# A hybrid attention encoder block: one 128-row transfer for each Q head, both key copies taken from the rotary tile

## The chip, the core and the metric

The kernel runs on one core of one Trainium2 chip. A core has a matrix engine (TensorE, PE in the profile, with its weight loads as PEld), a vector engine (DVE), a scalar engine (ACT), GpSimd (POOL) and SyncE (SP), which here only issues transfers. Sixteen DMA engines carry the transfers. The metric is the device time of one execution in microseconds (us), as the median of several runs.

## The reference, cut to what matters

One encoder layer of width 1024 over 512 tokens and 16 learned meta tokens (528 positions). All arithmetic is float32.

```python
u = rms_norm(h, pre_mix_gain[l])
proj = u @ w_in[l]
qa, ka, va, qb, kb, vb, g = jnp.split(proj, SPLITS, axis=-1)
qa = rope(qa.reshape(B, Lp, SWA_Q_HEADS, HEAD_DIM), pos)     # 16 heads of 64
ka = rope(ka.reshape(B, Lp, SWA_KV_HEADS, HEAD_DIM), pos)    # 4 key heads
qb = rope(qb.reshape(B, Lp, DIFF_HEADS, 2, HEAD_DIM), pos)   # 8 heads of 2 x 64
kb = rope(kb.reshape(B, Lp, DIFF_HEADS, 2, HEAD_DIM), pos)
o_swa = windowed_gqa_sink_attention(qa, ka, va, attn_sink[l], pos, is_real)
o_diff = differential_attention(qb, kb, vb, lam, lambda_init, diff_subln_gain[l], is_key)
gates = jax.nn.sigmoid(g + b_gate[l])
merged = g_swa * (o_swa @ w_branch_swa[l]) + g_diff * (o_diff @ w_branch_diff[l])
h = h + rms_norm(merged @ w_out[l], post_mix_gain[l])
u = rms_norm(h, pre_ffn_gain[l])
gate_up = u @ w_ffn_in[l]
f = (jax.nn.silu(gate_up[..., :D_FF]) * gate_up[..., D_FF:]) @ w_ffn_out[l]
h = h + rms_norm(f, post_ffn_gain[l])
```

The rotary embedding `rope` splits the 64 channels of a head into two halves of 32 and returns `x1*cos - x2*sin` and `x2*cos + x1*sin`. The windowed attention gives each query the keys within 128 positions, the meta keys and a sink logit. The differential attention subtracts one softmax from another over all keys.

## The kernel before, in words

To keep float32 accuracy every operand of a matmul is split into a high part and a rest (`hi`, `lo`), and a product is three matmuls: hi by hi, lo by hi, hi by lo (lines 286 to 288, `mm3`). A projection of 128 output channels over 512 tokens is 8 blocks of the contraction, so 24 matmuls, into one of three PSUM banks named `pr`. Its weights come as one transfer of 512 KB into `wr` (line 519), are cast to `wh` on ACT (L521) and subtracted to `wl` on DVE or POOL (L252).

For the attention scores the split is folded into the contraction: a head has 64 channels, a score matmul contracts over 128 rows, so the Q tile holds 128 rows, the hi and the lo part of each of the two rotary halves (4 blocks of 32 rows), and K holds the same key channels twice, once under the hi rows of Q and once under the lo rows, with a second index x for the hi and lo part of K. Two matmuls (x = 0, 1) give the score.

These rows come about as follows. `rope_t` (line 539) makes a tile `hl` for four heads at once: partition 32*head + channel, then the rotary half i, the part (hi or lo) and the token. DVE makes the products `ta` and `tb` (L546), POOL adds them (L558), ACT writes the hi part (L554), DVE the lo part (L550). There is one `hl` buffer, so the next rotary tile may write it only when all transfers out of it have landed. Then `move` (line 567) copies rows from SBUF to SBUF on SP's queue into K and Q:

- windowed keys, for each of 4 key heads: two transfers of 32 rows into the lower 64 rows of `KK`, and then one of 64 rows that copies `KK[0:64]` to `KK[64:128]`;
- windowed Q (`q_swa`, four groups of four heads): four transfers of 32 rows and 64 KB for each head;
- differential attention (`qk`, 8 heads of 2 components): for each component the same, two transfers of 32 rows and a copy of 64 rows for `Kd`, four transfers of 32 rows for `Qd`.

The order of the work from the projections to the end of the differential attention is a plan. Each step is entered as a task with its engine, a cost, the tiles that it reads and writes, and a priority (`Plan.task`). `Plan.run` goes through time and gives each engine the next ready task; what it emits is the engine's instruction order, which the hardware then follows. Within the plan a transfer costs SP 0.6 us and is done 2.7 us later (`land`; 4.0 for the copies of 64 rows), and two transfers into the same tile follow one another there; on the chip they don't wait for each other. Projection matmuls have the lowest rank for PE (`prio` from 20 up) and fill it wherever no attention step is ready. The tile pools have fixed counts: three `wr`, one `hl`, four `kk` (keys), eight `q`.

The attention stage runs from some 25 us to some 525 us of the span. In it the windowed attention (16 units of one query block of four heads: `s_swa`, scores into `Sw` at line 705 and softmax; `t_swa`, transposes at 754 and values into `O` at 761 and 764) comes first, then the differential attention (`s_diff`, scores into `Sd` at 853; `t_diff`). The output projections and the feed-forward part follow, in an order that the change doesn't touch.

Of the kernel before, what the change touches and what calls it, by code (L numbers as in the profile page):

```python
# [12 lines left out]
F32 = mybir.dt.float32  # L13
F32R = mybir.dt.float32r
# [222 lines left out]
def encoder(ctx, tc, I, out, dbg=None):  # L237
# [300 lines left out]

    def rope_t(hl, pa, pb, c0, n, p0, o0, scale, more=False):

# [8 lines left out]
        def low(o, n):  # L549
            dve.scalar_tensor_tensor(out=hl.t[:, :, 1, o:o + n], in0=ta.t[:, :, 0:n], scalar=scale,  # L550
                                     in1=hl.t[:, :, 0, o:o + n].bitcast(F32), op0=ALU.mult, op1=ALU.subtract)

        def high(o, n):
            act.activation(out=hl.t[:, :, 0, o:o + n], in_=ta.t[:, :, 0:n], func=AF.Copy, scale=scale)  # L554

# [11 lines left out]
    def move(out, in_, r, w, dep=(), land=2.7):  # L567
        return T("SP", 0.6, lambda: sp.dma_start(out=out().bitcast(F32), in_=in_().bitcast(F32)), r=r, w=w, dep=dep,
                 prio=2, land=land)

    X_ = []
# [78 lines left out]
    for g in range(4):  # L650
        K = sb("kk", [P, 2, KX], F32R, "KK", 4, zp)
        for i in range(2):
            move(lambda i=i, K=K: K.t[32 * i:32 * i + 32], lambda i=i, g=g: hk.t[32 * g:32 * g + 32, i], [hk], [K])
        move(lambda K=K: K.t[64:128], lambda K=K: K.t[0:64], [], [K], land=4.0)
        KB.append(K)
# [15 lines left out]
    def q_swa(g):  # L671
        dep = Ssteps[4 * g - 8][:1] if g >= 2 else ()
        wa, wb = weights(I["w_in"][4 + 2 * g], dep), weights(I["w_in"][5 + 2 * g], dep)
        late = Ssteps[4 * g - 7][-1:] if g >= 2 else ()
        pa, pb = products(wa, X, X_, NMETA, EXT, late), products(wb, X, X_, NMETA, EXT, late)
        hl = sb("hl", [P, 2, 2, KX], F32R, "hl", 1, zp)
        for s in range(2):
            rope_t(hl, pa, pb, NMETA + s * 256, 256, s * 256, s * 256, -0.125)
        QS[g] = [sb("q", [P, EXT], F32R, "Q", 8) for _ in range(4)]
        for hh in range(4):  # L680
            for i in range(2):
                for c in range(2):
                    b = 2 * c + i
                    move(lambda hh=hh, b=b: QS[g][hh].t[32 * b:32 * b + 32, 0:NTOK],
                         lambda hh=hh, i=i, c=c: hl.t[32 * hh:32 * hh + 32, i, c, 0:NTOK], [hl], [QS[g][hh]])

# [106 lines left out]
    def qk(h):  # L793
# [4 lines left out]
        wa, wb = weights(I["w_in"][12 + 3 * h], early), weights(I["w_in"][13 + 3 * h], early)  # L798
        hl = sb("hl", [P, 2, 2, KX], F32R, "hl", 1, zp)
        for s in range(2):  # L800
# [4 lines left out]
        for c in range(2):  # L805
            K = sb("kk", [P, 2, EXT], F32R, "Kd", 4, zp)
            Q = sb("q", [P, EXT], F32R, "Qd", 8)
            for i in range(2):
                move(lambda i=i, K=K: K.t[32 * i:32 * i + 32], lambda i=i, c=c: hl.t[64 + 32 * c:96 + 32 * c, i, :, 0:EXT],
                     [hl], [K])  # L810
            move(lambda K=K: K.t[64:128], lambda K=K: K.t[0:64], [], [K], land=4.0)
            for i in range(2):
                for x in range(2):
                    b = 2 * x + i
                    hd["moved"] = move(lambda b=b, Q=Q: Q.t[32 * b:32 * b + 32, 0:NTOK],
                         lambda i=i, x=x, c=c: hl.t[32 * c:32 * c + 32, i, x, NMETA:EXT], [hl], [Q])
            hd["Q"].append(Q)
            hd["K"].append(K)
# [59 lines left out]

    lnx, dd, results, B1 = [], [], [], []

    def t_diff(h):
# [4 lines left out]
        for kb in range(5):  # L886
# [17 lines left out]
            def high(kb=kb, ah=ah):  # L904
                for x in range(2):
                    pe.matmul(out=O.t, lhsT=V.t[:, x, kb], rhs=ah.t, start=(kb == 0 and x == 0), stop=False)  # L906
            hd["Av"].append(T("PE", 2 * mm_t(512), high, r=[ah, V], w=[O], prio=0))
            hd["Av"].append(T("PE", mm_t(512), lambda kb=kb, al=al: pe.matmul(
# [3 lines left out]
        ob, sq, sh, sl = rt("ob"), rt("sq"), rt("sh", F32R), rt("sl", F32R)  # L912
        T("ACT", 0.59, lambda: act.copy(out=ob.t, in_=O.t), r=[O], w=[ob], prio=0)
        T("ACT", 0.61, lambda: act.activation(out=sq.t, in_=O.t, func=AF.Square), r=[O], w=[sq], prio=0)
        T("ACT", 0.63, lambda: act.copy(out=sh.t, in_=sq.t), r=[sq], w=[sh], prio=2)
# [3 lines left out]
        def sums():  # L919
            pe.matmul(out=mp.t, lhsT=ones, rhs=sh.t, start=True, stop=False)  # L920
            pe.matmul(out=mp.t, lhsT=ones, rhs=sl.t, start=False, stop=True)
        T("PE", 2 * mm_t(512), sums, r=[sh, sl], w=[mp], prio=0)
        v, y, z = rt("v"), rt("y"), rt("z")
# [6 lines left out]
        T("ACT", 0.63, lambda: lnx.append(act.activation(out=y.t, in_=y.t, func=AF.Exp, scale=-0.5)), w=[y], prio=4)  # L930
        T("ACT", 0.63, lambda: act.activation(out=z.t, in_=y.t, func=AF.Square), r=[y], w=[z], prio=4)
        T("DVE", 0.69, lambda: dve.scalar_tensor_tensor(out=z.t, in0=z.t, scalar=-0.5, in1=v.t, op0=ALU.mult, op1=ALU.mult),
# [508 lines left out]
```

## Time and profile before

| | |
|---|---|
| median of 3 runs | 963.73 us (962.97 to 965.36) |
| the profiled execution: time | 965.27 us |
| the profiled execution: span from the first to the last instruction | 963.5 us |
| mean granted TensorE clock | 0.996 |
| busy: PE, PEld, DVE, ACT, POOL | 943.4, 844.1, 670.3, 504.3, 216.2 us |
| transfers | 109.43 MB, DMA engines busy 37.4% of the span |

The profile's page gives busy times, a timeline of 40 slices, a chain of waits that ended last, and groups of instructions. Further views are used below: who waited for whom; instructions in order of time; busy time by stretch, with the granted clock, the share of time in which the DMA engines were busy and what they moved; and transfers with the time from issue to landing. Times inside a view count from the start of the span. PE's ends are modelled, so a matmul's duration overlaps its successor; the distance between two starts is what a matmul costs.

### The profile page before, as it was taken

What the parts mean: (1) busy time and instruction counts of PE and PEld (TensorE: products, weight loads), DVE (VectorE), ACT (ScalarE), POOL (GpSimd) and SP (SyncE); (2) the same over time, 40 slices, a digit from 0 to 9 for tenths busy, and PEclk for the clock granted to TensorE, in tenths of its full rate; (3) what the DMA queues carried; (4) which work ended last, traced back from release to release, by engine and by line L of the source; (5) the groups of instructions that cost most, each with busy time, mean ns of one, the idle gap of its engine ahead of it and who ended that gap; (6) DMA issues with size and microseconds to landing.
All of it is one profiled execution on the core that took longest, in us unless ns stands there. A gap on an engine that the chain in (4) does not pass through costs nothing.

```text
span 963.5 us, 15670 instructions
## 1 busy us (share of the span) xinstructions
PE 943.4 (98%) x5919; PEld 844.1 (88%) x5919; DVE 670.3 (70%) x1202; ACT 504.3 (52%) x939; POOL 216.2 (22%) x228
## 2 busy tenths in 40 slices
PE   9898999999999999999999999999999999999996
PEld 9787878889898999999888888998999999988885
DVE  5836898999574759877774857877788788752224
ACT  6336676775644446667546433744555556632121
POOL 0543455543222323234212311300000000000000
PEclk9999999999999999999999999999999999999998
DMA  9483222251425144433531551444333332324122
GB/s 338 139 194 90 77 77 70 73 134 48 130 88 155 45 124 121 129 84 107 159 118 45 185 186 44 132 154 153 91 114 104 110 111 68 109 88 152 44 66 88
DMA packets 37147, 109.43 MB, mean 114 GB/s; under 512 B 6080, under 2 KB 6592, under 8 KB 37072
## 3 DMA queue, kind: packets, MB, share of 16 engines
q1 hardware_dynamic: 37072, 108.43, 37.4%
q8 instruction: 47, 0.77, 0.3%
q14 instruction: 28, 0.23, 0.1%
HBM read 87.04 MB, written 2.10 MB: 93 GB/s over the span
## 4 chain that ended last, share of the span: by engine, by line
PE 88%; DVE 5%; DMA 2%; ACT 1%; SPq 1%; issue 1%; DVEq 0%; ACTq 0%
PE pr L286 19%; PE pr L287 19%; PE pr L288 19%; PE Sd L853 3%; PE wk L287 2%; PE wk L288 2%; PE wk L286 2%; PE Sw L705 2%; PE O L761 2%; PE tr L893 2%; PE Od L906 2%; PE tr L288 2%; PE tr L287 2%; PE tr L286 2%; PE tr L754 2%; PE acc L288 1%
## 5 line engine op out<-in xcount | busy, mean ns | idle before, releaser
L286 PE MATMUL pr<-xh,wh 128*128 128x264 f32 (+1 forms) x616 | 199.9, 325 | 0.0
L288 PE MATMUL pr<-xh,wl 128*128 128x264 f32 (+1 forms) x616 | 196.5, 319 | 0.3 <-POOL wl L252 0.3
L287 PE MATMUL pr<-xl,wh 128*128 128x264 f32 (+1 forms) x616 | 196.6, 319 | 0.1
L252 POOL TENSOR_TENSOR wl<-wr,wh 128x1024 fp32r<-128x1024 f32 (+2 forms) x42 | 99.8, 2377 | 141.3 <-ACT wh L521 78.0
L252 DVE TENSOR_TENSOR wl<-wr,wh 128x1024 fp32r<-128x1024 f32 (+2 forms) x76 | 91.5, 1208 | 53.5 <-ACT wh L271 43.7
L288 PEld LDWEIGHTS pr<-xh,wl 128*128 128x128 f32 x616 | 116.0, 188 | 8.9 <-POOL wl L252 0.5
L287 PEld LDWEIGHTS pr<-xl,wh 128*128 128x128 f32 x616 | 116.2, 189 | 7.9 <-DVE xl L393 0.5
L286 PEld LDWEIGHTS pr<-xh,wh 128*128 128x128 f32 x616 | 116.3, 189 | 7.3
L521 ACT CAST wh<-wr 128x1024 fp32r<-128x1024 f32 x56 | 58.5, 1049 | 42.1 <-PE pr L287 34.5
L271 ACT CAST wh<-wr 128x1024 fp32r<-128x1024 f32 x44 | 46.2, 1052 | 65.3 <-PE pr L288 17.9
L308 POOL TENSOR_TENSOR r3y<-r3v,mhalf 128x1 f32<-128x1 f32 x4 | 2.2, 548 | 336.8 <-DVE r3v L307 336.8
L286 PE MATMUL pr<-TM,sx 128*128 128x256 f32 x240 | 68.1, 284 | 0.9 <-ACT u L1272 0.5
L287 PE MATMUL pr<-TM,sx 128*128 128x256 f32 x240 | 67.9, 283 | 0.0
L288 PE MATMUL pr<-TM,sx 128*128 128x256 f32 x240 | 67.9, 283 | 0.0
L858 DVE TENSOR_REDUCE nm<-Sd 128x1 f32<-128x528 f32 x64 | 45.1, 705 | 21.0 <-PE Sd L853 20.1
L288 PE MATMUL pr<-uh,wl 128*128 128x256 f32 (+1 forms) x200 | 59.2, 296 | 0.4 <-DVE wl L252 0.4
L286 PE MATMUL pr<-uh,wh 128*128 128x256 f32 (+1 forms) x200 | 59.3, 296 | 0.0
L287 PE MATMUL pr<-ul,wh 128*128 128x256 f32 (+1 forms) x200 | 59.1, 296 | 0.0
L252 DVE TENSOR_TENSOR sx<-S,sx 128x1024 fp32r<-128x1024 f32 x34 | 41.6, 1225 | 25.1 <-PE wk L287 12.7
L558 POOL TENSOR_TENSOR ta<-ta,tb 128x528 f32<-128x528 f32 (+1 forms) x26 | 36.5, 1402 | 79.1 <-DVE tb L546 59.3
L256 ACT CAST sx<-S 128x1024 fp32r<-128x1024 f32 x34 | 35.7, 1050 | 25.8 <-PE pr L288 8.1
L861 ACT ACTIVATE pp<-Sd,nm 128x528 f32<-128x528 f32 x40 | 28.0, 699 | 39.2 <-DVE pa L874 22.6
(401 smaller groups left out, 2550.1 us busy)
## 6 DMA issues: line engine op xcount, KB each, us to landing
wr<-in_w_in_dram SPq DMA_DIRECT2D x50, 512.0 KB, 4.2
wr<-in_w_fo_dram SPq DMA_DIRECT2D x22, 512.0 KB, 3.5
wg<-in_w_fi_dram SPq DMA_DIRECT2D x17, 512.0 KB, 3.6
wu<-in_w_fi_dram SPq DMA_DIRECT2D x17, 512.0 KB, 3.6
wr<-in_w_fi_dram SPq DMA_DIRECT2D x16, 512.0 KB, 4.2
Kd<-hl SPq DMA_DIRECT2D x32, 132.0 KB, 2.4
Kd<-Kd SPq DMA_DIRECT2D x16, 264.0 KB, 3.6
Q<-hl SPq DMA_DIRECT2D x64, 64.0 KB, 2.7
```

What stands on the lines that cost most here:

```text
L252: (eng or dve).tensor_tensor(out=lo, in0=src, in1=hi.bitcast(F32), op=ALU.subtract)
L256: act.copy(out=hi, in_=src)
L271: act.copy(out=wh, in_=raw)
L286: pe.matmul(out=ps, lhsT=ah, rhs=bh, start=first, stop=False, **more)
L287: pe.matmul(out=ps, lhsT=ah, rhs=bl, start=False, stop=False, **more)
L288: pe.matmul(out=ps, lhsT=al, rhs=bh, start=False, stop=last, **more)
L521: T("ACT", 1.05, lambda: act.copy(out=wh.t, in_=wr.t), r=[wr], w=[wh], prio=pr_)
L558: T("POOL", 0.05 + 1.3 * m, lambda: pool.tensor_tensor(out=ta.t[:, :, 0:n], in0=ta.t[:, :, 0:n], in1=tb.t[:, :, 0:n], op=ALU.add), r=[tb], ...
L705: pe.matmul(out=Sw2[S.slot][:, 0:nk], lhsT=QS[g][hh].t[:, i * P:(i + 1) * P], rhs=KB[g].t[:, x, r0:r1], start=(x == 0), stop=(x == 1))
L853: pe.matmul(out=S.t[:, s, 0:HALF], lhsT=Q[c].t[:, i * P:(i + 1) * P], rhs=K[c].t[:, x, s * HALF:(s + 1) * HALF], start=(x == 0), stop=(x = ...
L858: T("DVE", 0.71, lambda S=S, c=c, one=one: dve.tensor_reduce(out=nm.t[:, c, one], in_=S.t[:, :, 0:HALF], axis=AX.XY, op=ALU.min), r=[S], w ...
L861: T("ACT", 0.9, lambda S=S, c=c, one=one, p=p: act.activation(out=p().rearrange("p (a b) -> p a b", a=2), in_=S.t[:, :, 0:HALF], func=AF.E ...
```

## The change

It does four things.

1. In `q_swa` the rotary tile is laid out with the part (hi, lo) ahead of the rotary half (`hi_first`), so that the four pieces of a channel lie behind each other, and a head's Q becomes one transfer: 32 partitions of four pieces of 2 KB in the source, 128 rows of 2 KB in the destination. Row 4p + 2a + b of Q then holds piece (a, b) of channel p. In `qk` the same is done with the half ahead of the part.
2. Both copies of the windowed keys are written straight from `hl`. For each half i one transfer writes the 64 rows i, i+2, i+4, ... of `KK`; its source of 32 rows is read twice over (a broadcast). The copy from `KK` to `KK` is gone: per key head two transfers instead of three.
3. For the differential keys four transfers of 32 rows, each into every fourth row, replace two of 32 rows and the copy of 64. The tile `hl` is 528 wide there instead of 544, so a source row is contiguous (4224 bytes instead of two pieces of 2112).
4. In `t_diff` three tasks get further dependencies in the plan: the value matmuls of a head come after the previous head's `mp` matmuls, and the two ACT reads of `Od` after the previous head's last `z`. They bound the plan's order.

The plan's costs for a transfer stay as they were (0.6 us and 2.7 us to landing), so the plan itself comes out differently, and the order of instructions on all engines between the projections and the end of the differential attention with it.

```diff
-    def rope_t(hl, pa, pb, c0, n, p0, o0, scale, more=False):
+    def rope_t(hl, pa, pb, c0, n, p0, o0, scale, more=False, hi_first=False):
+
+        def part(x):
+            return hl.t[:, x] if hi_first else hl.t[:, :, x]
...
-            dve.scalar_tensor_tensor(out=hl.t[:, :, 1, o:o + n], in0=ta.t[:, :, 0:n], scalar=scale,
-                                     in1=hl.t[:, :, 0, o:o + n].bitcast(F32), op0=ALU.mult, op1=ALU.subtract)
+            dve.scalar_tensor_tensor(out=part(1)[:, :, o:o + n], in0=ta.t[:, :, 0:n], scalar=scale,
+                                     in1=part(0)[:, :, o:o + n].bitcast(F32), op0=ALU.mult, op1=ALU.subtract)
...
+    def move_q(Q, src, r):
+        return move(lambda: Q.t[:, 0:NTOK], lambda: src().rearrange("p a b c -> p (a b) c"), r, [Q])
...
         K = sb("kk", [P, 2, KX], F32R, "KK", 4, zp)
         for i in range(2):
-            move(lambda i=i, K=K: K.t[32 * i:32 * i + 32], lambda i=i, g=g: hk.t[32 * g:32 * g + 32, i], [hk], [K])
-        move(lambda K=K: K.t[64:128], lambda K=K: K.t[0:64], [], [K], land=4.0)
+            move(lambda K=K, i=i: K.t[i::2].rearrange("p x c -> p (x c)"),
+                 lambda g=g, i=i: hk.t[32 * g:32 * g + 32, i].rearrange("p x c -> p (x c)").unsqueeze(1).broadcast_to(
+                     [32, 2, 2 * KX]), [hk], [K])
...
-            rope_t(hl, pa, pb, NMETA + s * 256, 256, s * 256, s * 256, -0.125)
+            rope_t(hl, pa, pb, NMETA + s * 256, 256, s * 256, s * 256, -0.125, hi_first=True)
         QS[g] = [sb("q", [P, EXT], F32R, "Q", 8) for _ in range(4)]
         for hh in range(4):
-            for i in range(2):
-                for c in range(2):
-                    b = 2 * c + i
-                    move(lambda hh=hh, b=b: QS[g][hh].t[32 * b:32 * b + 32, 0:NTOK],
-                         lambda hh=hh, i=i, c=c: hl.t[32 * hh:32 * hh + 32, i, c, 0:NTOK], [hl], [QS[g][hh]])
+            move_q(QS[g][hh], lambda hh=hh: hl.t[32 * hh:32 * hh + 32, :, :, 0:NTOK], [hl])
...
-        hl = sb("hl", [P, 2, 2, KX], F32R, "hl", 1, zp)
+        hl = sb("hl", [P, 2, 2, EXT], F32R, "hl", 1, zp)
...
             for i in range(2):
-                move(lambda i=i, K=K: K.t[32 * i:32 * i + 32], lambda i=i, c=c: hl.t[64 + 32 * c:96 + 32 * c, i, :, 0:EXT],
-                     [hl], [K])
-            move(lambda K=K: K.t[64:128], lambda K=K: K.t[0:64], [], [K], land=4.0)
-            for i in range(2):
-                for x in range(2):
-                    b = 2 * x + i
-                    hd["moved"] = move(lambda b=b, Q=Q: Q.t[32 * b:32 * b + 32, 0:NTOK],
-                         lambda i=i, x=x, c=c: hl.t[32 * c:32 * c + 32, i, x, NMETA:EXT], [hl], [Q])
+                for a in range(2):
+                    move(lambda K=K, i=i, a=a: K.t[2 * i + a::4], lambda i=i, c=c: hl.t[64 + 32 * c:96 + 32 * c, i],
+                         [hl], [K])
+            hd["moved"] = move_q(Q, lambda c=c: hl.t[32 * c:32 * c + 32, :, :, NMETA:EXT], [hl])
...
-            hd["Av"].append(T("PE", 2 * mm_t(512), high, r=[ah, V], w=[O], prio=0))
+            hd["Av"].append(T("PE", 2 * mm_t(512), high, r=[ah, V], w=[O], dep=ms[-1:], prio=0))
...
-        T("ACT", 0.59, lambda: act.copy(out=ob.t, in_=O.t), r=[O], w=[ob], prio=0)
-        T("ACT", 0.61, lambda: act.activation(out=sq.t, in_=O.t, func=AF.Square), r=[O], w=[sq], prio=0)
+        T("ACT", 0.59, lambda: act.copy(out=ob.t, in_=O.t), r=[O], w=[ob], dep=zs[-1:], prio=0)
+        T("ACT", 0.61, lambda: act.activation(out=sq.t, in_=O.t, func=AF.Square), r=[O], w=[sq], dep=zs[-1:], prio=0)
...
-        T("PE", 2 * mm_t(512), sums, r=[sh, sl], w=[mp], prio=0)
+        ms.append(T("PE", 2 * mm_t(512), sums, r=[sh, sl], w=[mp], prio=0))
...
-        T("ACT", 0.63, lambda: act.activation(out=z.t, in_=y.t, func=AF.Square), r=[y], w=[z], prio=4)
+        zs.append(T("ACT", 0.63, lambda: act.activation(out=z.t, in_=y.t, func=AF.Square), r=[y], w=[z], prio=4))
```

The instruction orders of the two programs show where this moves work. Two engines matter for what follows. SP first: its queue from the windowed keys on, before. `KK` is a key tile, `wr` a weight tile, `Q` a query tile, `hl` the rotary tile; a row ends with rows by elements of the destination and the number of such transfers.

```order
L568 DMA KK<-hl 32x1088 x4
L519 DMA wr<-in_w_in_dram 128x1024
L568 DMA KK<-hl 32x1088 x4
L568 DMA KK<-KK 64x1088 x4
L519 DMA wr<-in_w_in_dram 128x1024 x2
L568 DMA Q<-hl 32x512 x8
```

And the same stretch of SP's queue with the change.

```order
L571 DMA KK<-hl 64x1x1088 x4
L519 DMA wr<-in_w_in_dram 128x1024
L571 DMA KK<-hl 64x1x1088 x4
L519 DMA wr<-in_w_in_dram 128x1024 x2
L571 DMA Q<-hl 128x1x512 x4
```

The four copies from `KK` are gone, each of the eight transfers out of `hl` writes 64 rows instead of 32, and the four heads' Q are four transfers where sixteen stood (the other eight of them stand further down, between weight loads).

On PE, the place where the windowed scores begin. `pr` rows are projection matmuls, `Sw` rows are scores. Before:

```order
L286 MATMUL pr<-xh,wh 128x512
L287 MATMUL pr<-xl,wh 128x512
L288 MATMUL pr<-xh,wl 128x512
L705 MATMUL Sw<-KK,Q 128x272 x4
L286 MATMUL pr<-xh,wh 128x512
L287 MATMUL pr<-xl,wh 128x512
```

With the change:

```order
L288 MATMUL pr<-xh,wl 128x512
L708 MATMUL Sw<-KK,Q 128x272 x2
L708 MATMUL Sw<-KK,Q 128x400 x2
L286 MATMUL pr<-xh,wh 128x512
L287 MATMUL pr<-xl,wh 128x512
L288 MATMUL pr<-xh,wl 128x512
L708 MATMUL Sw<-KK,Q 128x272 x4
```

The first score row stands at number 472 of PE's list before and at 427 with the change: 45 projection matmuls of 512 columns that stood ahead of the scores now stand behind their start. The first scores now take the first head for two query blocks, and the next group of scores takes the second and the third head, one projection block later. PE's list has the same matmuls in both programs. Before the first differential score 642 projection matmuls stand in both, counted from the start of the program.

More of the change, by code (lines that the diff above doesn't have):

```diff
@@ L549, in low @@
         def low(o, n):
-            dve.scalar_tensor_tensor(out=hl.t[:, :, 1, o:o + n], in0=ta.t[:, :, 0:n], scalar=scale,
-                                     in1=hl.t[:, :, 0, o:o + n].bitcast(F32), op0=ALU.mult, op1=ALU.subtract)
+            dve.scalar_tensor_tensor(out=part(1)[:, :, o:o + n], in0=ta.t[:, :, 0:n], scalar=scale,
+                                     in1=part(0)[:, :, o:o + n].bitcast(F32), op0=ALU.mult, op1=ALU.subtract)
         def high(o, n):
-            act.activation(out=hl.t[:, :, 0, o:o + n], in_=ta.t[:, :, 0:n], func=AF.Copy, scale=scale)
+            act.activation(out=part(0)[:, :, o:o + n], in_=ta.t[:, :, 0:n], func=AF.Copy, scale=scale)
         T("DVE", 0.15 + 0.55 * m, lambda: half(ta, pa, 1), r=[pa, ROT], w=[ta], prio=3)
@@ L877, in s_diff @@
         hd["a"], hd["A"], hd["keep"] = a, A, [pa, pp[0]]
-    lnx, dd, results, B1 = [], [], [], []
+    lnx, dd, results, B1, zs, ms = [], [], [], [], [], []
     def t_diff(h):
```

## Prediction

> **What bounds the kernel now.** I read the page's busy times first, then who waited for whom on PE.
>
> ```profile
> span 963.5 us, 15670 instructions
> PE 943.4 (98%) x5919; PEld 844.1 (88%) x5919; DVE 670.3 (70%) x1202; ACT 504.3 (52%) x939; POOL 216.2 (22%) x228
> ```
>
> PE is busy for all but 20 us, and its list of matmuls is the same in both programs. So the change can only win what PE waits, and lose what it makes PE wait. The waits of PE over the whole span, longest first (us in total, times, longest):
>
> ```profile
> PE Sw L705 <- DMA Q<-hl: 3.7, 1, 3.7
> PE tr L598 <- DVE VT L580: 2.8, 3, 1.6
> ```
>
> One wait is on a transfer of this change: the first windowed score waits 3.7 us for Q. None is on `Qd` or `Kd`. The same view from 77 to 530 us, the rest of the stage that is planned anew:
>
> ```profile
> PE Sd L853 <- ACT pp L861: 0.7, 1, 0.7
> PE tr L598 <- DVE VT L580: 0.5, 1, 0.5
> PE tr L754 <- DVE bdm L745: 0.5, 1, 0.5
> PE pr L288 <- POOL wl L252: 0.3, 1, 0.3
> PE O L761 <- DVE al L252: 0.2, 1, 0.2
> PE tr L754 <- DVE al L252: 0.2, 1, 0.2
> ```
>
> That is 2.4 us in all, none of it behind a transfer (and of the 2.8 us on `VT` above, 2.3 lie earlier, ahead of the change). PE around the one wait, in order of time (start, duration):
>
> ```profile
> 71.69 0.39 PE L286 MATMUL pr<-xh,wh 128*128 128x512 f32 x1
> 71.92 0.39 PE L287 MATMUL pr<-xl,wh 128*128 128x512 f32 x1
> 72.16 0.40 PE L288 MATMUL pr<-xh,wl 128*128 128x512 f32 x1
> 76.28 0.91 PE L705 MATMUL Sw<-KK,Q 128*128 128x272 f32 x4 [3.73 <-DMA Q<-hl]
> ```
>
> A projection matmul of 512 columns starts every 0.23 us; the gap runs from 72.5 to 76.3. Its price is more than the gap. Stretches of the span (length, busy time of PE, PEld, DVE, ACT, POOL, granted clock, DMA share, GB/s):
>
> ```profile
> 46.00:54.00 8.00, 8.00 (x36) 6.51 (x35) 2.09 (x3) 1.42 (x2) 4.91 (x3) 1.00 0.91 201
> 54.00:56.00 2.00, 2.00 (x11) 1.61 (x10) 1.23 (x1) 0.69 (x1) 0.00 (x1) 1.00 0.19 44
> ...
> 58.00:62.00 4.00, 4.00 (x19) 3.23 (x18) 2.74 (x5) 1.05 (x1) 1.05 (x1) 1.00 0.99 209
> ...
> 78.00:82.00 4.00, 4.00 (x15) 3.56 (x14) 2.28 (x10) 2.69 (x9) 0.97 (x2) 0.60 0.00 0
> ```
>
> After the gap the granted clock is 0.60 over 4 us; that costs 0.4 x 4 = 1.6 us. The whole place is worth 3.7 + 1.6 = 5.3 us. The Trainium skill (TensorE: Matmul & The Clock Gate, Part 1) says that the clock falls to half after a window of about 3.4 us without work and returns after a busy one; the row agrees, and no run here shows how short a gap leaves it alone.
>
> **Why Q is late.** SP's queue from the keys on (start, duration), then ACT's first step of Q with what ended its wait, then DVE behind it:
>
> ```profile
> 44.88 2.49 SPq L568 DMA_DIRECT2D KK<-hl  x4
> 47.48 0.52 SPq L519 DMA_DIRECT2D wr<-in_w_in_dram  x1
> 48.03 2.42 SPq L568 DMA_DIRECT2D KK<-hl  x4
> 55.79 3.25 SPq L568 DMA_DIRECT2D KK<-KK  x4
> 59.09 2.68 SPq L519 DMA_DIRECT2D wr<-in_w_in_dram  x2
> 61.81 6.09 SPq L568 DMA_DIRECT2D Q<-hl  x8
> ...
> 71.90 2.41 SPq L568 DMA_DIRECT2D Q<-hl  x4
> ```
>
> ```profile
> 56.80 1.16 ACT L554 ACTIVATE hl<-ta 128x512 fp32r<-128x512 f32 x2 [2.12 <-DMA KK<-hl]
> ```
>
> ```profile
> 57.47 0.69 DVE L550 SCALAR_TENSOR_TENSOR hl<-ta,hl 128x512 fp32r<-128x512 f32 x1 [1.53 <-ACT hl L554]
> 58.20 0.69 DVE L546 TENSOR_TENSOR ta<-pr,rot 128x512 f32<-128x512 f32 x1
> 58.80 0.68 DVE L550 SCALAR_TENSOR_TENSOR hl<-ta,hl 128x512 fp32r<-128x512 f32 x1
> ```
>
> The keys leave `hl` from 44.9 us, and ACT may write the first Q group into it only when all eight have landed, at 56.8. The tile is complete at 59.5, 2.7 us later. Then SP needs until 74.3 to issue sixteen pieces, with weight loads in between; the first head's last piece is the thirteenth, issued at 71.9.
>
> **The change part by part, first the issue times.** Transfers by kind (min, median and max of SP's time in ns):
>
> ```profile
> L568 SPq DMA_DIRECT2D Q<-hl x64: 507/588/1637, 61.8 to 173.6; - x64
> ...
> L568 SPq DMA_DIRECT2D KK<-KK x4: 515/606/1246, 55.8 to 57.8; - x4
> ```
>
> With 32 rows or 64 a move costs SP about 0.6 us, so I take 0.6 for a transfer of 128 rows. That shape is not in the trace; its bounds are 0.5 (the shortest row) and 4 x 0.6 = 2.4 us (as much as the four that it replaces). SP saves 84 of its 188 moves, 50 us, but it isn't what PE waits for except at this place. What counts is when the first head's Q lands, and which matmul PE has reached by then.
>
> PE gets there earlier: 45 projection matmuls move behind the first score, 45 x 0.23 = 10.4 us, so PE arrives at 72.5 - 10.4 = 62.1.
>
> Q cannot come 10 us earlier, because `hl` isn't free sooner. The eight key transfers out of `hl` now carry 272 KB each instead of 136: 8 x 272 KB and the weight load between them are 2.75 MB, where it was 1.64. In the stretch of 46 to 54 us the DMA engines were 91% busy and moved 201 GB/s; from 58 to 62 us, with transfers of 64 rows (`KK` to `KK`) and a weight load, 209 GB/s at 99%. So I take them as the limit: 46.0 + 2.75 MB / 205 GB/s = 59.4, and 0.6 us to the last receipt: `hl` free at **60.0** instead of 56.8. Bounds: 56.8 (the doubled rows cost nothing) and 62.1 (the tail that the rows show between 54.2, when 1.64 MB at 201 GB/s are done, and 56.8 comes on top of 59.4). With 2.7 us for the two rotary steps the first Q is issued at 62.7. The landings (count, KB each, median us from issue) of the transfers issued from 85 to 95 us, and then of two groups from 44 to 56 us:
>
> ```profile
> Q<-hl SPq DMA_DIRECT2D x12, 64.0 KB, 2.0
> ```
>
> ```profile
> KK<-hl SPq DMA_DIRECT2D x8, 136.0 KB, 5.2
> ...
> KK<-KK SPq DMA_DIRECT2D x1, 272.0 KB, 3.0
> ```
>
> 256 KB in 128 rows is nearest to the last, 3.0 us; bounds 2.0 (the 64 KB row) and 5.2 (behind other traffic). Q of the first head lands at **65.7**, where PE has been since 62.1: a wait of **3.6 us**, against 3.7 before. The second, third and fourth head follow at 256 KB / 209 GB/s = 1.25 us each; PE wants the second and third about 1.4 us after the first score and the fourth at 2.5, so the third is about 1 us late and the fourth another 0.2: **1.2 us** that weren't there (before, these heads' last pieces were issued only 0.6 us apart). The clock then falls as before: no difference. At this place the change costs 3.6 + 1.2 - 3.7 = +1.1 us. The gain in issue time is eaten by the earlier arrival of PE and the longer hold on `hl`.
>
> **The rest.** The score units now start about 10 us earlier on the clock (65.7 for 76.3), with 45 more projection matmuls left to fill PE behind them; I take half of the 2.4 us of waits from 77 us on as gone: **-1.2 us**, with 0 and -2.4 as bounds (and new ones of the same size if the new order fits worse, +2.4). From the first differential score on both programs have the same count of projection matmuls ahead, so nothing carries over. The differential K and Q cost 10 moves instead of 14 for a head, 2.4 us less of SP, and the copy's landing less. PE's rows show no wait there, so this is worth 0; projection matmuls cover it, and if they ran out at a head it would be those 2.4 us. `hi_first` changes addresses, not sizes: 0. The dependencies in `t_diff` put no wait into an instruction that the rows show as late: 0.
>
> **Sum**, against the profiled execution (965.3 us, span 963.5): +1.1 - 1.2 = -0.1 us. That execution is 1.5 us above the median of the three, so the forecast as a median is **963.6 us**. The likeliest case reaches from 961.0 to 966.0, by its bounds for the waits that follow and for Q's landing. A difference below 0.3%, 2.9 us, can't be told from none here.
>
> **Rivals.**
>
> *The key copies are not limited by the DMA engines* (chance 0.25, faster). For it: the share falls to 0.19 in the row from 54 to 56 us, so the engines had room before `hl` came free, and the wider destination may spread the writes; against it: 209 GB/s at 99% with 64-row transfers. Then `hl` is free at 56.8 as before, Q lands at 56.8 + 2.7 + 3.0 = 62.5, PE waits 0.4 + 1.2, the clock stays up: 1.6 - 3.7 - 1.6 - 1.2 = -4.9 us, **958.8**. The Trainium skill (DMA: Bandwidth & Descriptors, Where 436 GB/s comes from) says that transfers inside SBUF are bound by the fabric at 435 GB/s, by which the keys would take half of my time and this rival would hold; the 209 GB/s row speaks against it.
>
> *The new order spares more than half of the later waits* and also the drop of the clock, with the forecast's first wait (0.07, faster): -1.6 - 2.4 + 1.1, **960.8**, just at the bound of what can be told; I count it as faster.
>
> *`hl` is held until 62 us or longer* (0.19, slower). A broadcast source feeds twice the rows, and the weight load in the middle leaves a tail. Then Q lands at 62.1 + 2.7 + 3.0 = 67.8, PE waits 5.7 + 1.2 = 6.9, 3.2 more than before, and softmax and transposes of the first units are as late, so the -1.2 is lost: **966.9**. It decides for slower from `hl` free at about 61.8 on. For it: the last key transfer landed 6.9 us after its issue (49.9 to 56.8); against: that tail was there while the engines were idle, so more data may fit into it.
>
> *The 128-row transfer isn't one* (0.03, slower): SP takes 2.4 us for each, Q of the first head lands 1.8 us and of the fourth 7.2 us later: near **971**.
>
> **Chances.** The forecast, no change, has 0.46. Faster: 0.25 + 0.07 = 0.32; slower: 0.19 + 0.03 = 0.22. The range runs from the first rival's 958.8, a little below it for the rest of the waits, to the third's 966.9: 958.2 to 967.2.
>
> **What would show it.** Right: PE's longest wait is again the first `Sw` on `Q`, now near 62 us and 3 to 4.5 us long, with short ones on the next heads; ACT's first `hl` step of Q starts at 59 to 61 us; the granted clock falls again behind it; the `KK` moves move 200 to 215 GB/s; a Q move costs SP 0.5 to 0.7 us. Wrong: ACT starts that step at 57 us or before (the first rival), or after 61.8 (the third); Q moves of over 1 us on SP; a clock at 1.00 all through; new waits on PE of over 1 us in the differential stage.

## The result, and the profile after

The changed kernel takes 970.28 us (median of 6 runs, 969.42 to 972.64); the kernel before, run beside it, 963.35 us (6 runs, 960.92 to 965.36). The ratio is 1.0077, 95% interval 1.0061 to 1.0092: slower by some 7 us, where no change was forecast, and outside the range of 958.2 to 967.2.

The profiled execution of the changed kernel took 970.7 us, its span is 968.7. The profile of before that the prediction shows (965.3 us, span 963.5) was a long one for that kernel. So the kernel before was profiled once more (963.75 us, span 962.0, the last experiment group below), and the comparison by stage uses that one: the spans then differ by 6.7 us, about as the medians do.

The waits of PE in the changed kernel, over the whole span (engine, tile and line waited for, then us in total, times, longest):

```profile
PE Sw L708 <- DMA Q<-hl: 6.1, 4, 4.2
PE tr L604 <- DVE VT L586: 2.8, 3, 1.6
PE Sd L852 <- ACT pp L860: 1.7, 2, 1.5
PE tr L757 <- DVE aTm L748: 1.1, 2, 0.8
```

The first is the wait on `Q`: 6.1 us in four waits, where the second profile of before has one of 2.8. The third and fourth are small waits of before, grown (0.9 and 0.5 us there). The first score in the changed kernel, on PE's timeline (start, duration, and in brackets the idle time ahead with what ended it):

```profile
61.57 0.39 PE L288 MATMUL pr<-xh,wl 128*128 128x512 f32 x1
66.17 1.49 PE L708 MATMUL Sw<-KK,Q 128*128 128x272 f32 x4 [4.21 <-DMA Q<-hl]
67.46 0.63 PE L286 MATMUL pr<-xh,wh 128*128 128x512 f32 x1
...
68.74 1.11 PE L708 MATMUL Sw<-KK,Q 128*128 128x272 f32 x4
```

PE is free at 62.0 (66.17 less 4.21), where the forecast had it (62.1), and waits until 66.2. The matmul behind the score takes 0.63 us where it took 0.39: half clock. Two heads of the third group of `Q` are late too, from another stretch of that timeline:

```profile
142.53 0.52 PE L708 MATMUL Sw<-KK,Q 128*128 128x272 f32 x2 [0.75 <-DMA Q<-hl]
144.79 0.49 PE L708 MATMUL Sw<-KK,Q 128*128 128x272 f32 x2 [0.79 <-DMA Q<-hl]
```

Now the span by stage: length of the stretch, busy time of PE, PEld, DVE, ACT, POOL, then granted clock, DMA share, GB/s. First the kernel before, in its second profile:

```profile
0.00:50.00 50.00, 44.94 (x318) 40.69 (x319) 33.74 (x56) 25.16 (x42) 15.30 (x26) 0.97 0.68 233
62.00:77.00 15.00, 12.18 (x54) 9.62 (x54) 3.30 (x4) 3.35 (x4) 6.76 (x4) 1.00 0.83 215
77.00:150.00 73.00, 72.71 (x375) 59.12 (x374) 63.00 (x172) 50.89 (x129) 31.61 (x53) 1.00 0.29 78
150.00:225.00 75.00, 74.00 (x483) 66.03 (x482) 69.49 (x183) 55.69 (x142) 38.44 (x56) 1.00 0.33 86
225.00:300.00 75.00, 74.28 (x476) 66.35 (x475) 50.91 (x92) 40.35 (x74) 21.67 (x14) 1.00 0.36 96
300.00:525.00 225.00, 223.89 (x1461) 201.68 (x1460) 155.71 (x291) 130.03 (x244) 66.07 (x48) 1.00 0.40 110
```

And the changed kernel:

```profile
0.00:50.00 50.00, 45.65 (x325) 41.63 (x326) 34.17 (x56) 25.55 (x42) 16.37 (x27) 1.00 0.70 235
62.00:77.00 15.00, 10.83 (x46) 9.36 (x47) 9.15 (x28) 7.12 (x21) 9.09 (x11) 0.77 0.43 105
77.00:150.00 73.00, 70.31 (x361) 56.93 (x360) 63.36 (x171) 51.63 (x129) 31.00 (x53) 1.00 0.29 80
150.00:225.00 75.00, 73.67 (x448) 63.64 (x447) 63.39 (x160) 49.94 (x122) 34.50 (x49) 1.00 0.31 85
225.00:300.00 75.00, 74.79 (x500) 68.18 (x499) 49.78 (x90) 40.79 (x73) 23.11 (x16) 1.00 0.30 87
300.00:525.00 225.00, 222.27 (x1455) 200.32 (x1455) 156.67 (x291) 129.40 (x246) 64.17 (x47) 1.00 0.38 113
```

Length minus PE's busy time is what PE lost to waiting. At the place of the first scores (62 to 77 us) that is 2.82 us before and 4.17 after, +1.35; the clock there is 0.77, which the trace puts as 6.83 us at half speed, 4.95 of them behind the wait's end, some 2.5 us of work lost. From 77 to 525 us the four rows give 0.29 + 1.00 + 0.72 + 1.11 = **3.12 us** before and 2.69 + 1.33 + 0.21 + 2.73 = **6.96 us** after, +3.84. Against that the start (0 to 50 us) was better in this execution: 0.71 us less idle, and the stretch of 3.41 us at half clock (the 0.97; 1.7 us of work lost) isn't there: -2.4 us in all. The sum, 1.35 + 2.5 + 3.84 - 2.4 = 5.3, leaves 1.4 of the 6.7 us unplaced.

So there are two parts of about equal size: the place of the first scores, which the prediction watched, and smaller waits over the next 450 us, which it had put at a gain of 1.2. Of these later waits the longest in the changed kernel, from 77 to 530 us, are:

```profile
PE Sw L708 <- DMA Q<-hl: 1.9, 3, 0.8
PE Sd L852 <- ACT pp L860: 1.7, 2, 1.5
PE tr L757 <- DVE aTm L748: 1.1, 2, 0.8
```

Behind its first score the kernel before has no wait on `Q` at all. So 1.9 of the 3.84 us are later heads' `Q`, which lands 4.8 us after its issue (shown below) where the plan counts 2.7; some 0.8 are the softmax step `pp`, 0.6 the step `aTm`.

### The profile page after: what moved, and what is told of

The parts are those of the page before. It is cut to its first block, busy times and chain, and to the rows that moved or that the text cites. A ratio compares the mean times of both kernels' runs of the same rounds, so it can differ in the third digit from the quotient of the medians.

```text
span 968.7 us, 15539 instructions
## 1 busy us (share of the span) xinstructions
PE 945.0 (98%) x5919; PEld 845.1 (87%) x5919; DVE 672.5 (69%) x1202; ACT 505.4 (52%) x939; POOL 215.2 (22%) x228
## 4 chain that ended last, share of the span: by engine, by line
PE 87%; DVE 6%; DMA 2%; ACT 2%; issue 1%; SPq 1%; DVEq 0%; ACTq 0%; POOL 0%
PE pr L286 19%; PE pr L287 19%; PE pr L288 19%; PE Sd L852 3%; PE wk L288 2%; PE wk L287 2%; PE wk L286 2%; PE Sw L708 2%; PE tr L892 2%; PE Od L905 2%; PE tr L288 2%; PE tr L287 2%; PE tr L286 2%; PE O L764 2%; PE tr L757 1%; PE acc L287 1%
```

## The experiments

Two theories were tried against each other first: "order" (the plan counts a transfer as 2.7 us long, moves the first score 45 matmuls forward, and PE waits there for `Q`) and "transfers" (the doubled key traffic and the transfer of 128 rows are dear by themselves). After the first four runs "order" split in two: "place" (the loss is at the first score) and "re-plan" (any new order of this program has more waits, all along).

### The new transfers in the order of before

The plan of before is kept, task for task. Where a transfer of before has no counterpart, its task stays in the plan and issues nothing; the first of four pieces of Q issues the whole.

```diff
-                    move(... Q rows 32*b to 32*b+32 ...)
+                    def fn(...):
+                        if (i, c) == (0, 0):
+                            dma(QS[g][hh].t[:, 0:NTOK], hl...)      # 128 rows
+                    move_fn(fn, [hl], [QS[g][hh]])                  # same task in the plan
...
-        move(lambda K=K: K.t[64:128], lambda K=K: K.t[0:64], [], [K], land=4.0)
+        move_fn(lambda: None, [], [K], land=4.0)
```

> All transfers of the change (one transfer for each Q, both key copies straight from the rotary tile), but PE, DVE, ACT and POOL run their instructions in the order of the kernel before: the plan still counts four tasks for a Q and three for a K, of which some issue nothing. Theory of the order (the change loses because the plan counts a transfer as landed after 2.7 us, moves the first score 45 projection matmuls up, and PE then waits for Q): PE arrives at the first score at 72.5 us, Q landed near 66, so no wait there and no drop of the clock: 3.7 + 1.6 us less than before, about 958 us (956.5 to 960.5). Theory of the transfers (the doubled key traffic and the 128-row transfer are dear by themselves, in any order): 966 to 971 us.

Measured: 960.97 us (11 runs) against 962.39 of before (21 runs): ratio 0.9984, 0.9975 to 0.9993. PE's list has no wait on `Q` at all. The stretches of this kernel:

```profile
62.00:77.00 15.00, 15.00 (x70) 12.35 (x69) 9.31 (x18) 6.85 (x14) 8.40 (x5) 1.00 0.63 168
77.00:150.00 73.00, 72.70 (x373) 59.05 (x373) 63.24 (x173) 51.01 (x130) 31.89 (x54) 1.00 0.27 80
150.00:225.00 75.00, 74.00 (x491) 66.55 (x490) 69.67 (x181) 55.86 (x141) 40.33 (x58) 1.00 0.32 86
225.00:300.00 75.00, 74.30 (x467) 66.07 (x466) 50.45 (x87) 39.24 (x69) 20.71 (x13) 1.00 0.37 106
300.00:525.00 225.00, 223.90 (x1461) 201.61 (x1460) 156.61 (x290) 130.57 (x244) 67.25 (x49) 1.00 0.37 107
```

The place costs nothing, and from 77 to 525 us PE waits 0.30 + 1.00 + 0.70 + 1.10 = 3.10 us, as before. What the change was written for is worth 1.4 us, and the whole loss, 970.28 against 960.97, is the order's: PE, DVE, ACT and POOL issue their instructions in exactly the order of before, and the transfers are those of the change. "Transfers" falls. The gain is smaller than the 4 to 5 us expected; one reason is that the second profile of before loses 2.8 us at its first score and not 5.3.

### Only the keys new, in the order of before

As above, but Q in its four pieces (to every fourth row of the tile, as the new layout wants).

```diff
-                    move(lambda hh=hh, b=b: QS[g][hh].t[32 * b:32 * b + 32, 0:NTOK],
+                    move(lambda hh=hh, b=b: QS[g][hh].t[b::4, 0:NTOK],
```

> Order of all compute engines as before, the keys written straight from the rotary tile as in the change, Q in four pieces as before (each into every fourth row, so that the rows match). Theory of the order: the rotary tile comes free near 59.6 instead of 56.8 us, but SP is ready for Q near 62.4 instead of 61.8, so the first score waits 3.5 to 4.5 us as before: 962.5 to 965.5 us, no difference to before. Theory of the transfers, if the doubled key traffic is the dear part: 966 us or more.

Measured: 962.79 us, ratio 1.0000 (0.9991 to 1.0009): the time is as expected, the mechanism isn't. PE waits 1.6 us for `Q` at the first score, where 3.5 to 4.5 were expected, with no fall of the clock behind it (in an execution of 960.83 us, the shortest of the eleven). The single transfer of Q is worth 1.8 us beside the run above, the new keys nothing.

### The new order with Q in four pieces

```diff
     def move_q(Q, src, r):
-        return move(lambda: Q.t[:, 0:NTOK], ...)
+        def fn():
+            for b in range(4):
+                sp.dma_start(out=Q.t[b::4, 0:NTOK]..., in_=src()[:, b // 2, b % 2]...)
+        return T("SP", 0.6, fn, r=r, w=[Q], prio=2, land=2.7)
```

> The changed kernel with its order on all engines, but each Q in four transfers of 32 rows again (into every fourth row). Theory of the order: the first head's four pieces land near 66.3 us, like the one transfer; the next heads follow 2.5 us apart instead of 1.2 on average, so the fourth is some 5 us later than with single transfers: 972 to 976 us. Theory of the transfers, if the 128-row transfer is the dear part: faster than the changed kernel, 964 to 967 us.

Measured: 984.47 us, ratio 1.0227 (1.0213 to 1.0241). The direction was right, the size wasn't: PE waits for `Q` nine times, 12.8 us in all, not only at the first head. Under the new order the single transfer saves 14 us; under the old one 1.8.

### The plan told how long a transfer takes

```diff
-        return move(..., r, [Q])
+        return move(..., r, [Q], cost=1.1, land=3.0)
...
-                     [32, 2, 2 * KX]), [hk], [K])
+                     [32, 2, 2 * KX]), [hk], [K], cost=1.3, land=4.0)
```

> The changed kernel, and in the plan the transfers cost what they were seen to cost: a windowed key transfer 1.3 us of SP and 4.0 to landing, a Q 1.1 and 3.0 (0.6 and 2.7 before). The plan makes a new order; the first score stands 36 projection matmuls later than in the changed kernel. Theory of the order: PE arrives at 61.8 + 36 x 0.23 = 70.1 us, Q is there, the wait of 4.2, most of the three later waits on Q (1.9) and the half clock (about 3) go: 961 to 964 us. Theory of the transfers: within 2 us of the changed kernel, 968 to 972 us.

Measured: 967.68 us, ratio 1.0052 (1.0040 to 1.0065): missed, it lies between the two ranges. The wait for `Q` is gone, and these stand in PE's list in its place:

```profile
PE Sd L852 <- ACT pp L860: 5.9, 5, 2.2
...
PE Sw L708 <- DVE nm L711: 1.5, 2, 1.4
```

Here the theory that all the loss sits at the first score broke. "Re-plan" was formed on it, and the next four runs set it against "place".

### Other numbers in the plan

One number each: the landing that the plan counts for a move. (The expectations count PE's rows from three rows further ahead than the section on the change does; the differences are the same.) First for the changed kernel, 4.7 us instead of 2.7 (the measured landing of Q is 4.8, below).

```diff
-    def move(out, in_, r, w, dep=(), land=2.7):
+    def move(out, in_, r, w, dep=(), land=4.7):
```

> The changed kernel with one number of the plan changed: each transfer of keys and Q is counted as landing 4.7 us after its issue instead of 2.7 (the measured landing of Q). The first score then stands 33 rows later on PE (row 463 instead of 430; before 475), 7.6 us of projection matmuls at 0.23 us each, more than the 4.2 us of wait. Theory 'place': the wait of 4.2 us and 2.5 us of half clock go, the later groups of Q don't wait either (1.9 us): 962 us (961 to 964). Theory 're-plan': the new order makes other waits, as in the run where the plan knew a landing of 3.0 to 4.0 us: 967 us (965 to 969), with waits of the scores on their softmax steps in its list.

Measured: 981.30 us, ratio 1.0185 (1.0167 to 1.0204). The place is clean, as the row from 62 to 77 us shows, and the order behind it is far worse:

```profile
62.00:77.00 15.00, 15.00 (x71) 12.46 (x71) 11.37 (x26) 7.13 (x19) 7.31 (x6) 1.00 0.53 152
...
300.00:525.00 225.00, 209.81 (x1371) 189.43 (x1370) 152.50 (x281) 123.37 (x237) 59.61 (x46) 0.96 0.33 99
```

15.2 us of waiting in the differential stage, 12.8 of them (seven waits, the longest 4.4 us) of `Sd` on the softmax step `pp` on ACT.

Then the kernel before, all of its own transfers, with the same number moved by 0.2 us, down and up.

```diff
-    def move(out, in_, r, w, dep=(), land=2.7):
+    def move(out, in_, r, w, dep=(), land=2.5):      # the other run: 2.9
```

> The kernel before with one number of its plan changed: a transfer is counted as landing 2.5 us after its issue instead of 2.7; all transfers and all arithmetic are those of before. The first score stands 6 rows earlier on PE (469 instead of 475), 1.4 us. Theory 'place': the wait at the first score grows by 1.4 us, perhaps 0.5 us of half clock more: 964.8 us (964 to 966). Theory 're-plan': 2881 rows of PE's order differ, and the later waits change with them: 966 us (964 to 969), with later waits (from 77 to 530 us) that grow from 2.4 us to 5 or more.

> The kernel before with a landing of 2.9 us in its plan instead of 2.7, nothing else. The first score stands 3 rows later (478 instead of 475), 0.7 us. Theory 'place': the wait shrinks by 0.7 us: 962.7 us (962 to 963.5). Theory 're-plan': 965 us (963 to 968), later waits of 4 us or more from 77 to 530 us instead of 2.4.

Measured: 978.67 us with 2.5 (ratio 1.0161, 1.0141 to 1.0180) and 975.50 us with 2.9 (1.0137, 1.0117 to 1.0157). No transfer and no arithmetic differs from the kernel before. With 2.5 the first score waits 8.6 us. Two weight loads, where one stood before, now stand right ahead of the last four pieces of `Q` in SP's queue, and these pieces land 5.9 to 6.7 us after their issue instead of 3.4 to 4.2 (the profile puts the wait down to the load itself):

```profile
61.91 9.24 SPq L568 DMA_DIRECT2D Q<-hl  x12
71.25 1.38 SPq L519 DMA_DIRECT2D wr<-in_w_in_dram  x2
72.68 2.44 SPq L568 DMA_DIRECT2D Q<-hl  x4
```
With 2.9 that wait is 2.8 us, as "place" had it, and yet the kernel is 13 us slower. Its longest waits on PE, from 77 to 530 us:

```profile
PE Sd L853 <- ACT pp L861: 6.2, 6, 2.1
PE tr L893 <- DVE Vd L252: 1.5, 1, 1.5
PE Sd L853 <- DMA wr<-in_w_in_dram: 1.3, 1, 1.3
PE Od L898 <- ACT aTm L897: 1.3, 1, 1.3
PE pr L288 <- DVE wl L252: 1.2, 1, 1.2
PE Od L908 <- DVE dal L252: 1.0, 1, 1.0
```

"Re-plan" had all three slower than the kernel before, which they are; its sizes (965 to 967) were far too small.

And two small moves of the number in the changed kernel, 2.5 and 3.2, which leave the first score within 3 rows of where it was.

> The changed kernel with a landing of 2.5 us in its plan instead of 2.7, nothing else. The first score stands 3 rows earlier (427 instead of 430), 0.7 us; 2579 rows of PE's order differ behind it. Theory 'place': 971 us (970 to 972). Theory 're-plan': the later waits are drawn anew, and the time lies anywhere from 966 to 982 us, most likely 2 us or more away from 970.3, with the difference in waits behind 77 us.

> The changed kernel with a landing of 3.2 us in its plan instead of 2.7, nothing else. The first score stands 3 rows later (433 instead of 430), 0.7 us. Theory 'place': 969.6 us (968.6 to 970.6). Theory 're-plan': anywhere from 966 to 982 us, most likely 2 us or more away from 970.3.

Measured: 976.55 us (1.0139, 1.0124 to 1.0154) and 971.37 us (1.0090, 1.0076 to 1.0104). The first is 6 us from the changed kernel, outside what "place" allows. Part of that lies at the first score all the same: it waits 6.7 us instead of 4.2, where 0.7 more were expected. Behind it come 2.0 us more of later waits (9.0 for 7.0) and 6.83 us at half clock at 433 us. The second is 1.1 us away, which the intervals don't tell from nothing, so that it decides nothing between the theories; its waits are others, though: 3.9 us at the first score, then 2.1 us of a projection on `wl`.

### The gap at the first score filled

18 extra matmuls of 512 columns ahead of the first score, so that PE doesn't idle there.

```diff
+                for y in range(18 if (u, hh) == (0, 0) else 0):
+                    pe.matmul(out=Sw2[S.slot][:, 0:512], lhsT=X[0][:, 0, 0:P], rhs=X[0][:, 0, 0:512], start=True,
+                              stop=True)
```

> The changed kernel with 18 matmuls of 512 columns written ahead of the first windowed score on PE, into the bank that the score then overwrites, so that PE works through the 4.2 us in which it waits for Q; nothing else is moved. The work of the kernel is complete; the 18 are extra. Theory 'place' (the loss lies at the first score, wait and half clock): the extra matmuls fit the gap (18 x 0.23 = 4.1 us), the half clock behind it is gone, and about 2.5 us with it (the 4.95 us from 66.17 to 71.12 us that ran at half rate): 967.8 us (966.8 to 968.8), no clock drop between 60 and 80 us. Theory 're-plan' (the loss lies in many later waits of a new order, the place at the first score costs before and after alike) gives the same 2.5 us if the drop is gone; it loses if more than that comes back. If the clock falls in any case (a drop that the keys or the start owe), the time stays at 970.3.

Measured: 969.61 us, ratio 1.0066 (1.0051 to 1.0081): 0.7 us less than the changed kernel, where 2.5 were expected. The clock stays at 1.00 all through the place, and the wait of 4.2 us is filled; this row shows what is left there:

```profile
62.00:77.00 15.00, 14.16 (x67) 10.97 (x66) 9.86 (x29) 7.69 (x22) 9.47 (x11) 1.00 0.43 106
```

PE is still idle for 0.84 us: at full speed it comes to the next heads before their `Q` has landed, which at half speed it didn't. So of the 2.5 us some 1.7 could come back. With intervals of 1.4 us to each side the 0.7 isn't told apart from that, nor from nothing; the half clock is the smaller part of the 7 us in any case.

### The first group of heads without Q

The scores of the first four heads read a piece of the input instead of `Q`; every queue has the instructions of the changed kernel in its order.

```diff
-                    pe.matmul(out=Sw2[S.slot][:, 0:nk], lhsT=QS[g][hh].t[:, i * P:(i + 1) * P],
+                    pe.matmul(out=Sw2[S.slot][:, 0:nk], lhsT=(X[0][:, hh] if g == 0 else QS[g][hh].t)[:, i * P:(i + 1) * P],
```

> The changed kernel, its order on every engine and all its transfers untouched, but the windowed scores of the first four heads read a piece of the input xh instead of Q (so these heads' results are not the reference's); no score of the first group can wait for Q any more. Theory 'place': the whole loss sits there, and all of what PE loses at the first four heads goes (4.2 us of wait, the half clock behind it, the waits for the second to fourth head that the run with the filled gap showed: 7.0 us of lost time from 50 to 75 us against 0.6 us where nothing waits): 963.9 us (963 to 965), equal to the kernel before with its place, and 0.5 us above it. Theory 're-plan': what is then left above the same transfers under the old order (960.97 us) is the price of the new order's later waits: 3 us, no more and no less; if 961 comes out the later waits cost nothing, if 967 or more they are most of the loss.

Measured: 968.77 us, ratio 1.0064 (1.0052 to 1.0077). Only 1.5 us come back, where 6.4 were expected, and the intervals hardly tell the 1.5 from nothing. Another wait takes the place of the one on `Q`. PE, then DVE in the same microseconds:

```profile
63.50 0.40 PE L288 MATMUL pr<-xh,wl 128*128 128x512 f32 x1
66.24 1.11 PE L708 MATMUL Sw<-KK,xh 128*128 128x272 f32 x4 [2.35 <-DVE nm L711]
```

```profile
62.96 0.68 DVE L549 TENSOR_TENSOR tb<-pr,rot 128x512 f32<-128x512 f32 x1
65.08 0.69 DVE L549 TENSOR_TENSOR tb<-pr,rot 128x512 f32<-128x512 f32 x1 [1.44 <-POOL ta L561]
65.69 0.49 DVE L711 CUSTOM_DVE_ANT_0 p<-Sw,mk,nsink 128x272 f32<-128x272 f32 x1
```

The scores have two banks. The first two scores now run at 62.4, where they ran at 66.2; the third needs a bank back and so DVE's first softmax step. That stands in DVE's queue behind a rotary step of the second Q group, which waits until 65.1 for POOL. So the third score, at 68.7 in the changed kernel, could not have come before 66.2 even with every `Q` in place, and the clock falls for 3.4 us behind this gap too. The rows behind the place:

```profile
77.00:150.00 73.00, 70.49 (x362) 57.05 (x361) 63.44 (x171) 51.64 (x129) 31.12 (x53) 1.00 0.28 78
...
300.00:525.00 225.00, 222.27 (x1453) 200.31 (x1452) 156.69 (x291) 128.19 (x243) 65.18 (x48) 1.00 0.38 111
```

From 77 to 525 us PE waits 6.86 us, with the wait at the first head taken away; 6.96 in the changed kernel; 6.85 with the gap filled. So these waits follow neither from the gap nor from the half clock at the place, and they don't move with it: without `Q` the scores from the third on run some 2 us sooner. An earlier start by much more was not tried in this order. Two other orders, with next to nothing lost at the place, have more of them (the run with 4.7 above, and the one in which the plan knew the landing).

### The kernel before once more

> The kernel before, unchanged, profiled once more beside the three others, since its first profiled execution (965.3 us) lies some 2 us above the median of its runs. If the wait and the half clock at the first score (5.3 us by that first profile) belong to it always, the wait of 3.7 us stands here too and a clock drop behind it; if its usual execution is spared a part, the wait is there and the drop is not, and the time is 961 to 963 us.

Measured: 962.92 us (8 runs, beside 962.74). The wait at the first score is 2.8 us, and no clock drop lies behind it; the drop of 3.4 us lies at 38 us instead, behind the waits on `VT`. The 5.3 us that the prediction gave the place belong to the execution that was profiled first.

### All of them together

Lost time of PE (length minus busy, by the stretches shown above), in us; "old" order is that of the kernel before.

| kernel | order | transfers | ratio to before | 62 to 77 us | 77 to 525 us |
|---|---|---|---|---|---|
| before, second profile | old | old | 1.0003 | 2.8 | 3.1 |
| new transfers, old order | old | new | 0.9984 | 0.0 | 3.1 |
| new keys only, old order | old | keys new | 1.0000 | 1.6 | 3.2 |
| the change | new | new | 1.0077 | 4.2 | 7.0 |
| gap filled | as the change | new | 1.0066 | 0.8 | 6.9 |
| first group without Q | as the change | new | 1.0064 | 2.4 | 6.9 |
| four pieces | as the change | keys new | 1.0227 | 5.9 | 13.9 |
| plan knows 1.1/3.0 and 1.3/4.0 | another | new | 1.0052 | 0.9 | 9.1 |
| plan 2.5 | another | new | 1.0139 | 5.9 | 9.0 |
| plan 3.2 | another | new | 1.0090 | 3.9 | 7.8 |
| plan 4.7 | another | new | 1.0185 | 0.0 | 16.6 |
| before, plan 2.5 | another | old | 1.0161 | 5.9 | 12.2 |
| before, plan 2.9 | another | old | 1.0137 | 2.8 | 14.5 |

One order, three sets of transfers: 3.1 to 3.2 us from 77 us on. Seven other orders, whatever the transfers: 7 to 17 us (the one with four pieces left aside), and all seven slower than the kernel before, by 5 to 18 us. The stretches don't count what the half clock takes on top, so the columns don't add up to the ratios.

The best kernel of all is the first experiment: the transfers of the change in the order of before, 0.9984 of the kernel before and 9 us below the change.

## Why the prediction was wrong

**What it had right.** PE's arrival at the first score (62.1 forecast, 62.0 measured) and the time at which `hl` comes free. The keys are limited as it said; the changed kernel's row from 46 to 54 us:

```profile
46.00:54.00 8.00, 8.00 (x36) 6.46 (x36) 1.94 (x3) 1.58 (x2) 4.90 (x3) 1.00 0.90 209
```

209 GB/s at a share of 0.90; ACT's first step into `hl` started at 59.67 (60.0 forecast) and not at 57 or before, and the first Q was issued at 62.39 (62.7). So the rival that the keys are not limited is out. The 0.6 us to the last receipt in that forecast stand in no row; no run shows them apart. The Trainium skill (DMA: Bandwidth & Descriptors, Where 436 GB/s comes from) gives 435 GB/s for the fabric; these transfers of 32 source rows moved half of that, as they did before. The rival with `hl` held past 62 us is out too: slower, as it had it, came true by another cause. The transfer of 128 rows is one transfer. And the dependencies added in `t_diff` did nothing: without them the program is the same, instruction for instruction.

**Q's landing was mis-sized.** The forecast took 3.0 us for 256 KB, from one key copy of 64 rows. Landings in the changed kernel (count, KB each, median us from issue):

```profile
Q<-hl SPq DMA_DIRECT2D x16, 256.0 KB, 4.8
```

The first took 3.74 us (62.39 to 66.13), the other three of the group up to 4.9, and with no other traffic from 76 us on they took as long. The first move of a group costs SP 0.55 us of its queue, near the 0.6 counted, but four in a row take 4.20, up to 1.7 each. So the first wait is 4.2 for 3.6, and the bounds of 2.0 to 5.2 held it. The 1.2 us counted for the next heads did not come: PE, at half clock, reached them after their `Q` had landed, and with the gap filled they cost 0.8. The landing's larger price lies further on, in the 1.9 us of later waits on `Q`.

**"The clock then falls as before: no difference" failed.** It fell for 6.83 us where the profile of before had 3.41, and in the second profile of before it doesn't fall there at all. With the gap filled, 0.7 us came back, of some 1.7 that could. Of the place as a whole, +1.1 was forecast; the stage rows give 1.35 us of waiting and up to 2.5 of half clock.

**"The rest: -1.2 us" failed, and it takes the time out of the range.** The step took it that 45 projection matmuls more behind the scores would fill half of the later waits, and set +2.4 as its far bound. They filled none: the later waits went from 3.12 to 6.96 us, +3.84, while the same transfers in the old order have 3.10. The place and the rest are each about half of the loss. With this step alone at its measured +3.84 instead of -1.2 the forecast would have been 968.6, slower and past 967.2; with the place alone at its measured 1.35 + 2.5 instead of +1.1, 966.4, still within the range. Two of the forecast's signs of being wrong did appear: Q moves of over 1 us on SP, and in the differential stage a new wait of over 1 us (1.5, of `Sd` on `pp`).

**The missing rival.** The list had "the new order spares more" at 0.07. That the new order fits worse stood only in the far bound of +2.4, without a chance or a time of its own. The runs make that the likeliest case: of seven re-drawn orders seven are slower. The change's text is about transfers, but it takes tasks out of a plan that lays out some 500 us of work on five engines with one pass of a greedy rule; the gain of the transfers is 1.4 us, and this draw of the order costs some 9.

**What stays open.** Why the order of before fits so much better than all the others is not shown. If its plan's numbers had been picked as the best of many, seven worse draws of seven would be no surprise; how they were chosen isn't known. In the changed kernel half of the new later waits are on `Q`, whose landing the plan counts short; a plan that counts it longer loses these waits and gets others. In the runs where the plan counts 1.1/3.0 and 4.7, and in the kernel before with 2.9, the largest are `Sd` on `pp`, a softmax step on ACT (5.9, 13.1 and 6.2 us), so a count of the plan for that chain may be short as well, but no run changed that count. Nor is it shown which of the changed plan's early choices puts the 3.84 us there.

## What to carry to other kernels

Where a planner or a greedy rule writes out the order, an edit of any task is two changes: the work itself, and a new draw of the whole order. Cost them apart, and measure them apart: keep the old order with the new work (tasks left in the plan that issue nothing), and re-draw the order with the old work (one cost moved by a little). If the second spread is larger than the gain expected of the first, as here 13 to 16 us for 0.2 us in one constant against a gain of 1.4, the forecast is a forecast of the draw, and a well-fitted old order makes slower the likely side.

When a wait is to be priced, look for the second thing that is late at the same point: here the first scores were held by `Q` until 66.2 us, and the third would have been held by DVE's queue until the same time, so that with the wait on `Q` taken away, the one that the profile names, 1.5 us came back of its 4.2.

## What the runs showed of the hardware

- A transfer of 256 KB from 32 rows to 128 landed 3.7 to 5.2 us after its issue (median 4.8), and took SP 0.55 us as the first of a group and up to 1.8 behind others, 4.1 to 4.6 for four. Four pieces of 64 KB took SP 2.4 to 2.8 us in the same queue; they landed 2.0 us (median) after their issues from 85 us on in the kernel before, and 3.4 to 6.7 us in two groups that stood right behind weight loads (3.4 to 4.2 in the kernel before, 5.9 to 6.7 in its plan with 2.5).
- The clock fell to half for stretches of 3.41, 6.83 or 10.24 us, multiples of one length. Whether a gap is followed by one isn't decided by its length alone: a wait of 2.83 us at the first score left the clock at 1.00 in the kernel before, a wait of 2.8 us at the same score in its re-drawn order was followed by 3.4 us at half, and one of 2.35 us was enough in the run without Q. The Trainium skill (TensorE: Matmul & The Clock Gate, Part 1) says that the window is free-running, which fits: the same gap falls differently into it. It names a window of about 3.4 us without work as what halves the clock; here a gap of 2.35 us, with matmuls in the same 3.4 us, was enough.
